# Merged operands ahead of the norm's casts, and a last down step with all operands kept, its products by halves of the positions

## The chip, the core and the metric

The kernel runs on one core of one Trainium2 chip. The core has a matrix engine (TensorE, PE in the profile; its weight loads are listed apart as PEld), a vector engine (VectorE, DVE), a scalar engine (ScalarE, ACT), a general engine (GpSimd, POOL) and a queue engine that issues the DMA transfers here (SyncE, SP). Each engine works through its own instructions in the order of the program and waits on semaphores for the others. Two on-chip memories matter: SBUF for operands and PSUM, in banks, for the sums of the matmuls.

The metric is the device time of one execution in microseconds (us), lower being better. All times of one profile count from the start of its span, the time from the first to the last instruction.

## The reference

One layer of an encoder block on 1040 positions (16 meta tokens and 1024 of the input) of 1024 channels, in float32. Two token mixers are merged by gates, the result is projected, normed and added to the residual; then comes a gated feed-forward part with a depthwise convolution of three taps, normed and added too.

```python
gates = jax.nn.sigmoid((gate_logits + b_gates[l]).reshape(bn, L, N_BRANCHES, D_MODEL))
merged = gates[:, :, 0] * y_a + gates[:, :, 1] * y_b
mix_out = merged @ w_out[l]
h_res = h_res + rmsnorm(mix_out, g_mix_post[l])

h2 = rmsnorm(h_res, g_ffn_pre[l])
up = centred_dwconv(h2 @ w_up[l], conv_w_ffn[l], conv_b_ffn[l])
a, v = jnp.split(up, 2, axis=-1)
ffn_out = (jax.nn.gelu(a) * v) @ w_down[l]
h_res = h_res + rmsnorm(ffn_out, g_ffn_post[l])
```

The output is `h_res` without the 16 meta tokens.

## The kernel before

Channels lie on the 128 partitions, positions on the free axis. A float32 operand of a matmul is split into a high half, a cast to `float32r` on ACT (L132), and a low half, the operand minus its high half, on DVE (L133). `mm3` (L160 to L168) then makes three matmuls of a product: high weights by high operand (L164), high by low (L166), low by high (L168). One level of a Strassen-Winograd scheme makes the large products out of seven half-sized ones (steps 0 to 6).

Two places of the program are touched.

**The out projection** (`project`, L958 ff.) computes `merged @ w_out` in four chunks of 258, 258, 258 and 256 positions (`CHM`). A chunk has eight tiles of 128 output channels (`mo`), each a sum over eight input tiles `kt`, that is 24 matmuls. After each tile ACT squares it (`sq_m`, L929) and scales it out of PSUM into `hA` or `hB` (L983, the eviction); DVE adds the squares. Hooks after a tile issue other work. With chunk `c` these are:

- after tile 0 the loads of the merged values of chunk `c + 1` into the three raw buffers (`mr`, `load_merged`);
- after tile 1 `norm_a(c - 1)`: the root of the mean, the scaling, the residual and the squares of the next norm;
- after tile 5 the splits of the first three (`MORE`) of the next chunk's eight merged operands (`mh` and `ml`, `split_merged`);
- after tile 6 the mean of the second norm (`mean_b`, one pair of matmuls into `ms_h`) and `norm_b(c - 1)`: three steps on DVE for the inverse root, eight scalings (L1028) and four casts with subtractions into `b11` and `b21`, operands of the feed-forward part;
- after tile 7 the splits of the other five merged operands, ordered by `issue_after` behind the last cast of `b11` (`cast`, `last_parts`).

Chunk `c + 1` can begin with the first three operands and needs the fourth after nine matmuls.

**The down projection** runs its steps in the order 0, 2, 4, 1, 3, 5, 6. Every step is a sum over eleven `k` (`NK`) with four output tiles each: 44 products of three matmuls over 512 positions, with the sums of steps 4, 3 and 6 in the PSUM banks `dna`, of step 5 in `dnb`. `operands` loads the gated values of two `k` into a raw buffer (`g`, three buffers of 512 KB), and splits weights (`wd`) and values (`gd`) into a ring of seven slots, so splits run some three `k` ahead of PE. Weights lie in rooms, large tiles named by `places`, two per room.

Step 6 is the last. Its first seven `k` run over all 512 positions. The last four (`LATE`) are split into rooms of their own (`late`) and multiplied by halves of 256 positions (`CUT`), so that the first half is complete before the second. Positions are output in two halves of 512: `finish(1, ...)` scales the second half of the positions (`z12`, `z22`), adds the residual (`hr`) and stores, after the mean that PE makes behind `k = 1`; `finish(0, ...)` does so for the first half of the positions (`z11`, `dn_u`), in two parts of 256.

```python
    load_residual(1, NK + 1)
    down(6, A, range(2))
    end = finish(1, mean(1), [(V, f, 1) for f in range(KT)])
    down(6, A, range(2, NK - LATE))
```

A recording layer with its own scheduler sets the final order on each engine; `behind` (`issue_after`) puts a group of instructions behind a named one.

Of the kernel before, what the change touches and what calls it, by code (L numbers as in the profile page):

```python
# [91 lines left out]
def block_kernel(ctx, tc, xT, x_res, w_u, w_in, w_fa, w_fa2, w_fb, w_fb2, w_co, w_out, w_up, w_dn,  # L92
# [861 lines left out]
    def split_merged(c, ks):  # L954
        for kt in ks:
            merged[c].append(merged_parts(c, kt, merged_r[c, kt // 3 * 3][:, kt % 3])[0])

    def project(c, hooks, order=range(KT)):  # L958
        n = CHM[c][1]
        sq = squares(f"m{c}", n)  # L960
        next(sq)
        outs = {}

        ahead = 5 if c == 0 else 0

        def mm(f, kt):
            if f not in outs:
                outs[f] = bank(f"mo{c}_{f}")[:, :n]
            mh, ml = merged[c][kt]
            with behind(*newest):  # L970
                mm3([outs[f]], tuple(t[:, kt * P : (kt + 1) * P] for t in wres[f]), ([mh], [ml]), kt == 0, kt == KT - 1)

        with behind(*done):
            while len(wres) < KT:
                out_weights(len(wres))
        for f in range(ahead):
            for kt in range(KT - 1):
                mm(f, kt)
        for n_, f in enumerate(order):
            for kt in range(KT - 1 if f < ahead else 0, KT):  # L980
                mm(f, kt)
            sq.send(outs[f])
            S.mul(h_at(c, f), outs[f], col("g_post", f))  # L983
            if n_ in hooks:
                with behind(*newest):
                    hooks[n_]()
        z[c] = sq
# [32 lines left out]
    def norm_b(c):  # L1020
# [5 lines left out]
        for f in range(KT):  # L1026
            h = h_at(c, f)
            V.scalar_tensor_tensor(out=h, in0=h, scalar=col("g_fpre", f), in1=rr, op0=ALU.mult, op1=ALU.mult)  # L1028
            if f % 2 == 0:
                continue  # L1030
            f -= 1
            if c < 2:
                a, e = max(c0, 1), min(c0 + n, NH + 1)
                got = put2(
                    hx["b11" if f < 4 else "b21"], f % 4, hA[f // 4][:, f % 4 : f % 4 + 2, a:e], a - 1, e - a
                )
                cast[:] = got[:1] if f < 4 else cast
            elif f < 4:
                sub(A(f), h_two(c, f), A(f))
                put2(hx["t1"], f, A(f), c0 - 513, n)  # L1040
            else:
                put2(hx["b22"], f - 4, B(f), c0 - 513, n)


    cast = []

    def second(c):
        j, n = CHM[c][0] - 513, CHM[c][1]
# [165 lines left out]
        psum_s.close()  # L1214
        psum_s, psum = scope("psum3", 6, space=PSUM)

    def last_parts(c):

        with behind(*cast):
            split_merged(c, range(MORE, KT))  # L1220

    project(0, {
        3: lambda: load_merged(1), 4: new_banks, 5: lambda: split_merged(1, range(MORE)),
        7: lambda: last_parts(1),
    })
    for c in range(1, 4):
        hooks = {
            0: lambda: load_merged(c + 1), 1: lambda: norm_a(c - 1), 5: lambda: split_merged(c + 1, range(MORE)),
            6: lambda: (mean_b(c - 1), norm_b(c - 1)), 7: lambda: last_parts(c + 1),
        }  # L1230
        order = range(KT)
        if c == 3:
# [99 lines left out]
    ssum = [fn.tile([P, HALF], F32, name=f"ss{i}") for i in range(2)]  # L1332
    A = [bank(f"dna{f}", firsts_) for f in range(4)]
    B = [bank(f"dnb{f}", None if f < 2 else seconds) for f in range(4)]
    LATE = 4
    AHEAD = 3
    CUT = 256
    PART0 = [(V, f, 1) for f in range(KT)]
    PART1 = [(V, 6, 1), (V, 0, 1), (V, 1, 1), (V, 2, 2), (V, 7, 1), (V, 4, 2)]
    gs = {}  # L1340
    hr = []

    def scr(name):
        return fn.tile([P, HALF], F32, tag="rs", name=name, bufs=3)
# [62 lines left out]
        rsqrt_of(f"r4_{half}_{o}", scr, ms, n, rr)  # L1407
        return rr

    def load_residual(half, at):  # L1410
        hr[:] = [tiles_in(at + i, f"hr{half}{i}") for i in range(2)]
        h0 = NM - TM + half * HALF
        for i in range(2):
            at = 0
            for c in (2 * half, 2 * half + 1):
                a = h0 + at - CHM[c][0]
                n = min(CHM[c][1] - a, HALF - at)
                SP.dma_start(hr[i][:, :, at : at + n], hres_d[c, :, 4 * i : 4 * i + 4, a : a + n])
                at += n
            assert at == HALF  # L1420

    def finish(half, rr, work, o=0, n=HALF):

        at = slice(o, o + n)
        for e, f, m in work:
# [21 lines left out]
    for f in range(4):  # L1447
        add(z22[:, f], A[f], z22[:, f])
        square(1, f + 4, z22[:, f])
    down(5, B)  # L1450
    for f in range(4):
        add(z12[:, f], B[f], u[:, f])
        square(1, f, z12[:, f])
    load_residual(1, NK + 1)
    down(6, A, range(2))
    end = finish(1, mean(1), [(V, f, 1) for f in range(KT)])
    down(6, A, range(2, NK - LATE))
    late = []
    for k in range(NK - LATE, NK):
        r = room(places[k - NK + LATE], F32R, f"late{k}")  # L1460
        into = [(r[:, i : i + 512], r[:, i + 512 : i + 1024]) for i in (0, 1024)]
        late.append((k, *operands(6, k, into)))
    list(end)
    load_residual(0, LATE)
    end = iter(())
    for o, n in ((0, CUT), (CUT, HALF - CUT)):
        at = slice(o, o + n)
        for f in range(4):
            next(end, None)
            for k, w, g in late:  # L1470
                mm(6, A, f, k, w, g, at)
            summed = add(u[:, f, at], A[f][:, at], u[:, f, at])
            rest = square(0, f + 4, u[:, f, at], o, n, last=f == 3)
            if f == 3:
                rr = mean(0, o, n, [rest])
                S.mul(u[:, f, at], u[:, f, at], col("g_fpost", f + 4))
        with behind(summed):
            list(end)
        end = finish(0, rr, PART0 if o == 0 else PART1, o, n)
    list(end)  # L1480
    dn_s.close()
    hx_s.close()
# [105 lines left out]
```

## Time and profile before

| | |
|---|---|
| time, median of 3 runs | 1212.87 us (1210.99 to 1213.8) |
| profiled execution, its own time | 1209.85 us |
| its span, first to last instruction | 1207.9 us |
| mean granted TensorE clock | 0.988 |
| out projection (PE works on `mo`) | 422.6 to about 531 us |
| down projection, step 6 on PE | 1159.98 to 1192.65 us |

The profile is of one execution. A row of a timeline gives the start, the duration, the engine, the line of the kernel, the operation, the tile written and the tiles read (buffer numbers left out), the shape, and in brackets the idle time of that engine just before, with what ended it. Rows of several equal instructions in a row are joined, with their count. A window's row gives the busy time of each engine in it. Matmuls are pipelined: the distance between two starts is what one costs, and it is shorter than the duration of one.

### The profile page before, as it was taken

The page shows a single profiled execution, that of the slowest core. Times are in us where ns is not written, and L with a number is a line of the kernel's source. Part 1 is how long each engine was busy: PE and PEld are TensorE (multiplying, and loading weights), DVE is VectorE, ACT ScalarE, POOL GpSimd, SP SyncE. Part 2 cuts the span into 40 slices and gives each one's busy share as a digit, 9 for nine tenths or more (in the row PEclk, how much of TensorE's full clock was granted, in tenths as well). Part 3 has the DMA queues.
Part 4 walks back from the last instruction along what each step waited for, and adds up shares of the span by engine and source line. Part 5 has one row for each costly group of instructions (what it writes and reads, how often), then busy time and mean ns, then how long its engine had stood idle before and what let it go on. Part 6 is the DMA issues. An engine that isn't in the chain of part 4 may idle for free.

```text
span 1207.9 us, 22189 instructions
## 1 busy us (share of the span) xinstructions
PE 1176.8 (97%) x8790; PEld 1134.4 (94%) x8790; DVE 997.4 (83%) x1685; ACT 549.1 (45%) x988; POOL 8.7 (1%) x41
## 2 busy tenths in 40 slices
PE   8999999999999998899999999999999999999995
PEld 7999999999999998899999999999999998888884
DVE  8999876756588857799799999989988989856678
ACT  6743343223443254456544544444344444455562
POOL 0000000000020000000000000000000000000000
PEclk9999999999999998899999999999999999999998
DMA  6336655132967853334243334323212499354433
GB/s 250 123 119 216 194 172 172 57 128 91 293 214 235 273 152 110 108 107 163 97 138 108 117 129 149 123 97 132 97 71 96 137 330 317 101 167 125 136 119 140
DMA packets 79215, 184.26 MB, mean 153 GB/s; under 512 B 7954, under 2 KB 25586, under 8 KB 79112
## 3 DMA queue, kind: packets, MB, share of 16 engines
q1 hardware_dynamic: 78968, 182.73, 46.2%
q8 instruction: 69, 1.13, 0.4%
q14 instruction: 34, 0.28, 0.1%
q10 hardware_dynamic: 144, 0.12, 0.0%
HBM read 131.55 MB, written 51.27 MB: 151 GB/s over the span
## 4 chain that ended last, share of the span: by engine, by line
PE 52%; DVE 4%; ACT 1%; DMA 1%; issue 0%; DVEq 0%; SPq 0%; ACTq 0%
PE up_d L168 3%; PE up_c L166 3%; PE up_c L164 3%; PE up_d L164 3%; PE up_d L166 3%; PE up_c L168 3%; PE up_a L164 3%; PE up_a L168 3%; PE up_a L166 3%; PE dna L166 3%; PE dna L164 3%; PE dna L168 3%; PE dnb L166 2%; PE dnb L164 2%; PE dnb L168 2%; PE up_b L168 2%
## 5 line engine op out<-in xcount | busy, mean ns | idle before, releaser
L166 PE MATMUL mo<-ml,wo 128*128 128x258 f32 (+1 forms) x256 | 74.5, 291 | 6.0 <-DVE ml L133 6.0
L164 PE MATMUL mo<-mh,wo 128*128 128x258 f32 (+1 forms) x256 | 75.5, 295 | 2.5 <-ACT mh L132 2.5
L168 PE MATMUL mo<-mh,wo 128*128 128x258 f32 (+1 forms) x256 | 74.1, 289 | 0.0
L166 PEld LDWEIGHTS mo<-ml,wo 128*128 128x128 f32 x256 | 50.7, 198 | 6.5 <-DVE ml L133 6.3
L164 PEld LDWEIGHTS mo<-mh,wo 128*128 128x128 f32 x256 | 50.5, 197 | 3.1 <-ACT mh L132 2.9
L168 PEld LDWEIGHTS mo<-mh,wo 128*128 128x128 f32 x256 | 50.5, 197 | 0.0
L132 ACT CAST up_1h<-up_1t 128x512 fp32r<-128x512 f32 x11 | 6.8, 622 | 74.9 <-DVE up_1t L149 44.6
L1160 ACT ACTIVATE up_0o<-up_0o 128x512 f32<-128x512 f32 x44 | 27.8, 631 | 23.7 <-DVE up_0o L1158 23.4
L1156 ACT ACTIVATE up_1o<-up_1x,pr 128x512 f32<-128x512 f32 x33 | 26.9, 816 | 23.0 <-DVE up_1x L149 22.5
L168 PE MATMUL up_d<-b22h,up_5l 128*128 128x258 f32 (+1 forms) x168 | 34.2, 284 | 0.0
L166 PE MATMUL up_c<-t3l,up_3h 128*128 128x258 f32 (+1 forms) x168 | 34.1, 285 | 0.0
L168 PE MATMUL up_b<-t2h,up_2l 128*128 128x258 f32 (+1 forms) x168 | 34.0, 283 | 0.0
L164 PE MATMUL up_d<-b22h,up_5h 128*128 128x258 f32 (+1 forms) x168 | 33.9, 283 | 0.0
L166 PE MATMUL up_d<-b22l,up_5h 128*128 128x258 f32 (+1 forms) x168 | 33.9, 283 | 0.0
L166 PE MATMUL up_b<-t2l,up_2h 128*128 128x258 f32 (+1 forms) x168 | 33.9, 283 | 0.0
L164 PE MATMUL up_c<-t3h,up_3h 128*128 128x258 f32 (+1 forms) x168 | 33.8, 282 | 0.0
L164 PE MATMUL up_b<-t2h,up_2h 128*128 128x258 f32 (+1 forms) x168 | 33.8, 282 | 0.0
L164 PE MATMUL up_c<-t4h,up_6h 128*128 128x258 f32 (+1 forms) x168 | 33.8, 282 | 0.0
L164 PE MATMUL up_d<-t1h,up_1h 128*128 128x258 f32 (+1 forms) x168 | 33.7, 282 | 0.0
L168 PE MATMUL up_d<-t1h,up_1l 128*128 128x258 f32 (+1 forms) x168 | 33.7, 282 | 0.0
L168 PE MATMUL up_c<-t3h,up_3l 128*128 128x258 f32 (+1 forms) x168 | 33.6, 281 | 0.0
L166 PE MATMUL up_d<-t1l,up_1h 128*128 128x258 f32 (+1 forms) x168 | 33.6, 281 | 0.0
(1337 smaller groups left out, 4295.8 us busy)
## 6 DMA issues: line engine op xcount, KB each, us to landing
g<-gp_d SPq DMA_DIRECT2D x35, 512.0 KB, 3.6
up_1r<-in_w_up_dram SPq DMA_DIRECT2D x22, 512.0 KB, 3.6
gp_d<-up_0o SPq DMA_DIRECT2D x44, 256.0 KB, 2.0
up_0r<-in_w_up_dram SPq DMA_DIRECT2D x20, 512.0 KB, 3.9
s<-sig_d SPq DMA_DIRECT2D x16, 514.0 KB, 6.2
sig_d<-g_s SPq DMA_DIRECT2D x30, 257.0 KB, 3.4
u<-fold_d SPq DMA_DIRECT2D x8, 777.0 KB, 4.2
fold_d<-fold SPq DMA_DIRECT2D x8, 521.0 KB, 3.3
```

Source lines behind the costliest of these rows:

```text
L132: a = copy(hi, src)
L164: nc.tensor.matmul(o, wh, h, start=first, stop=False, **kw)
L166: nc.tensor.matmul(o, wh, l, start=False, stop=False, **kw)
L168: newest[:] = [nc.tensor.matmul(o, wl, h, start=False, stop=last, **kw).ins]
L1156: S.activation(t, ap[:, 1 : 1 + HALF], AF.Identity, bias=col("cb_ffn", b), scale=w(1))
L1160: S.activation(t, t, AF.Gelu_apprx_tanh)
```

## The change

Nothing of what is computed changes. In the out projection all eight splits of the next chunk's merged operands are issued before `norm_b`, the first three behind the eviction of tile 5 (hook 5), the other five behind the eviction of tile 6 (hook 6, between `mean_b` and `norm_b`). `last_parts` and `cast` go.

In the down projection all eleven pairs of step 6's operands are kept, ten in rooms and the last in the ring. Five are prepared among the `k` of step 5, as their rooms come free, two after it and the rest within step 6. Step 6 runs all its `k` over the first 256 positions for the four tiles together, then over the second 256 positions tile by tile, each tile with all eleven `k`. The `finish` of the second half of the positions is issued with one tile per `k`, and the first half's residual is loaded into a tile of its own (`hr00`) and one room. `finish(0, ...)` works on two tiles at a time for all tiles.

```diff
@@ project
-            S.mul(h_at(c, f), outs[f], col("g_post", f))
+            evicted[:] = [S.mul(h_at(c, f), outs[f], col("g_post", f)).ins]
...
-    def last_parts(c):
-
-        with behind(*cast):
-            split_merged(c, range(MORE, KT))
+    def parts(c, ks):
+
+        with behind(*evicted):
+            split_merged(c, ks)
...
-            0: lambda: load_merged(c + 1), 1: lambda: norm_a(c - 1), 5: lambda: split_merged(c + 1, range(MORE)),
-            6: lambda: (mean_b(c - 1), norm_b(c - 1)), 7: lambda: last_parts(c + 1),
+            0: lambda: load_merged(c + 1), 1: lambda: norm_a(c - 1), 5: lambda: parts(c + 1, range(MORE)),
+            6: lambda: (mean_b(c - 1), parts(c + 1, range(MORE, KT)), norm_b(c - 1)),
@@ down projection
-    LATE = 4
     AHEAD = 3
     CUT = 256
-    PART0 = [(V, f, 1) for f in range(KT)]
-    PART1 = [(V, 6, 1), (V, 0, 1), (V, 1, 1), (V, 2, 2), (V, 7, 1), (V, 4, 2)]
+
+    EASY = 5
+    TWOS = [(V, f, 2) for f in range(0, KT, 2)]
...
-    down(5, B)
+
+
+    late = []
+
+    def last_operands(k):
+        into = (None, None)
+        if k < NK - 1:
+            r = room(places[k], F32R, f"late{k}")
+            into = [(r[:, i : i + 512], r[:, i + 512 : i + 1024]) for i in (0, 1024)]
+        late.append(operands(6, k, into))
+
+    for k in range(NK):
+        down(5, B, [k])
+        if k % 2 and k // 2 < EASY:
+            last_operands(k // 2)
     for f in range(4):
         add(z12[:, f], B[f], u[:, f])
         square(1, f, z12[:, f])
-    load_residual(1, NK + 1)
-    down(6, A, range(2))
-    end = finish(1, mean(1), [(V, f, 1) for f in range(KT)])
-    down(6, A, range(2, NK - LATE))
-    late = []
-    for k in range(NK - LATE, NK):
-        r = room(places[k - NK + LATE], F32R, f"late{k}")
-        into = [(r[:, i : i + 512], r[:, i + 512 : i + 1024]) for i in (0, 1024)]
-        late.append((k, *operands(6, k, into)))
+    res = load_residual(1, [tiles_in(NK + 1 + i, f"hr1{i}") for i in range(2)])
+    last_operands(EASY)
+    last_operands(EASY + 1)
+    for k in range(NK):
+        if EASY + 1 < k + 2 < NK and k + 2 >= len(late):
+            last_operands(k + 2)
+        for f in range(4):
+            mm(6, A, f, k, *late[k], slice(0, CUT))
+        if k == 0:
+            end = finish(1, mean(1), [(V, f, 1) for f in range(KT)], res)
+        else:
+            next(end, None)
+        if k == 4:
+            res0 = load_residual(0, [fn.tile([P, 4, HALF], F32, name="hr00"), tiles_in(NK + 1, "hr01")])
     list(end)
-    load_residual(0, LATE)
     end = iter(())
     for o, n in ((0, CUT), (CUT, HALF - CUT)):
         at = slice(o, o + n)
         for f in range(4):
-            next(end, None)
-            for k, w, g in late:
-                mm(6, A, f, k, w, g, at)
-            summed = add(u[:, f, at], A[f][:, at], u[:, f, at])
+            if o:
+                for k in range(NK):
+                    mm(6, A, f, k, *late[k], at)
+            add(u[:, f, at], A[f][:, at], u[:, f, at])
             rest = square(0, f + 4, u[:, f, at], o, n, last=f == 3)
             if f == 3:
                 rr = mean(0, o, n, [rest])
                 S.mul(u[:, f, at], u[:, f, at], col("g_fpost", f + 4))
-        with behind(summed):
-            list(end)
-        end = finish(0, rr, PART0 if o == 0 else PART1, o, n)
+            else:
+                next(end, None)
+                next(end, None)
+        end = finish(0, rr, TWOS, res0, o, n)
     list(end)
```

What stands where on DVE at the end of chunk 1 of the out projection, before the change (`r3_0` and `rrb0` are the second norm of chunk 0, `sq_m1_7` the square of chunk 1's tile 7, `ml2_3` and on the low halves of chunk 2's operands):

```order
L174 SCALAR_TENSOR_TENSOR r3_0_t_5746<-r3_0_y_5745 128x258
L175 SCALAR_TENSOR_TENSOR r3_0_t_5746<-ms_h0_5742,r3_0_t_5746 128x258
L176 SCALAR_TENSOR_TENSOR rrb0_5744<-r3_0_t_5746,r3_0_y_5745 128x258
L1028 SCALAR_TENSOR_TENSOR hA0_5160<-hA0_5160,pr_67,rrb0_5744 128x258 x4
L133 TENSOR_TENSOR b11l_5167<-hA0_5160,b11h_5166 128x2x257
L1028 SCALAR_TENSOR_TENSOR hA1_5161<-hA1_5161,pr_67,rrb0_5744 128x258
L133 TENSOR_TENSOR b11l_5167<-hA0_5160,b11h_5166 128x2x257
L1028 SCALAR_TENSOR_TENSOR hA1_5161<-hA1_5161,pr_67,rrb0_5744 128x258 x3
L149 TENSOR_TENSOR sq_m1_0_5495<-sq_m1_0_5495,sq_m1_7_5792 128x258
L133 TENSOR_TENSOR b21l_5169<-hA1_5161,b21h_5168 128x2x257 x2
L133 TENSOR_TENSOR ml2_3_5797<-mr2_3_5500,mh2_3_5796 128x258
L133 TENSOR_TENSOR ml2_4_5801<-mr2_3_5500,mh2_4_5800 128x258
```

The same place of the changed program:

```order
L174 SCALAR_TENSOR_TENSOR r3_0_t_5766<-r3_0_y_5765 128x258
L133 TENSOR_TENSOR ml2_3_5745<-mr2_3_5500,mh2_3_5744 128x258
L133 TENSOR_TENSOR ml2_4_5749<-mr2_3_5500,mh2_4_5748 128x258
L133 TENSOR_TENSOR ml2_5_5753<-mr2_3_5500,mh2_5_5752 128x258
L133 TENSOR_TENSOR ml2_6_5757<-mr2_6_5502,mh2_6_5756 128x258
L133 TENSOR_TENSOR ml2_7_5761<-mr2_6_5502,mh2_7_5760 128x258
L175 SCALAR_TENSOR_TENSOR r3_0_t_5766<-ms_h0_5742,r3_0_t_5766 128x258
L176 SCALAR_TENSOR_TENSOR rrb0_5764<-r3_0_t_5766,r3_0_y_5765 128x258
L149 TENSOR_TENSOR sq_m1_0_5495<-sq_m1_0_5495,sq_m1_7_5812 128x258
L1031 SCALAR_TENSOR_TENSOR hA0_5160<-hA0_5160,pr_67,rrb0_5764 128x258 x4
L133 TENSOR_TENSOR b11l_5167<-hA0_5160,b11h_5166 128x2x257
```

The five subtractions have moved from behind the eight scalings and four subtractions of the norm to right behind its first step. At the start of chunk 3 it reads alike.

On PE, the mean of the second half of the positions (`ms4_1_0`) in step 6, before the change and, in the second fence, after it (`late2` holds the operands of `k = 2`):

```order
L164 MATMUL dna3_12106<-gd6_1h_13667,wd6_1h_13663 128x512
L166 MATMUL dna3_12106<-gd6_1l_13668,wd6_1h_13663 128x512
L168 MATMUL dna3_12106<-gd6_1h_13667,wd6_1l_13664 128x512
L1405 MATMUL ms4_1_0_13683<-ss1_12102,ones_69 128x512
L164 MATMUL dna0_12103<-gd6_2h_13699,wd6_2h_13695 128x512
```

```order
L168 MATMUL dna1_12104<-late2_13516 128x256
L164 MATMUL dna2_12105<-late2_13516 128x256
L1401 MATMUL ms4_1_0_13701<-ss1_12102,ones_69 128x512
L166 MATMUL dna2_12105<-late2_13516 128x256
L168 MATMUL dna2_12105<-late2_13516 128x256
```

The mean stood behind 24 matmuls of 512 positions and now stands behind 31 of 256.

On DVE, the end of step 5's splits before the change (`wd6_0` and on are the weights of step 6, `z12` the sum that closes step 5):

```order
L133 TENSOR_TENSOR wd5_10l_13594<-wd_b22h_12096,wd5_10h_13593 128x512
L133 TENSOR_TENSOR gd5_10l_13598<-g5_10_13590,gd5_10h_13597 128x512
L133 TENSOR_TENSOR wd6_0l_13643<-wd_t2l_12091,wd6_0h_13642 128x512
L133 TENSOR_TENSOR gd6_0l_13647<-g6_0_13639,gd6_0h_13646 128x512
L133 TENSOR_TENSOR wd6_1l_13664<-wd_t3h_12092,wd6_1h_13663 128x512
L133 TENSOR_TENSOR gd6_1l_13668<-g6_0_13639,gd6_1h_13667 128x512
L149 TENSOR_TENSOR z12_12097<-dnb0_12107,dn_u_12099 128x512
```

And after it:

```order
L133 TENSOR_TENSOR wd5_10l_13630<-wd_b22h_12096,wd5_10h_13629 128x512
L133 TENSOR_TENSOR late6_13681<-g6_6_13682,late6_13681 128x512
L133 TENSOR_TENSOR late7_13776<-g6_6_13682,late7_13776 128x512
L133 TENSOR_TENSOR gd5_10l_13634<-g5_10_13626,gd5_10h_13633 128x512
L133 TENSOR_TENSOR wd6_10l_13845<-wd_b22h_12096,wd6_10h_13844 128x512
L133 TENSOR_TENSOR late8_13797<-g6_8_13798,late8_13797 128x512
L133 TENSOR_TENSOR late9_13820<-g6_8_13798,late9_13820 128x512
L133 TENSOR_TENSOR gd6_10l_13849<-g6_10_13841,gd6_10h_13848 128x512
L149 TENSOR_TENSOR z12_12097<-dnb0_12107,dn_u_12099 128x512
```

Every operand of step 6 is now split before `z12`; no split is left between `z12` and the last store.

More of the change, by code (lines that the diff above doesn't have):

```diff
@@ L956, in split_merged @@
             merged[c].append(merged_parts(c, kt, merged_r[c, kt // 3 * 3][:, kt % 3])[0])
+    evicted = []
     def project(c, hooks, order=range(KT)):
@@ L1033, in norm_b @@
                 a, e = max(c0, 1), min(c0 + n, NH + 1)
[L1034 to L1037, printed above, removed]
+                put2(hx["b11" if f < 4 else "b21"], f % 4, hA[f // 4][:, f % 4 : f % 4 + 2, a:e], a - 1, e - a)
             elif f < 4:
@@ L1042, in norm_b @@
                 put2(hx["b22"], f - 4, B(f), c0 - 513, n)
-    cast = []
     def second(c):
@@ L1215, in new_banks @@
         psum_s, psum = scope("psum3", 6, space=PSUM)
-    def last_parts(c):
-        with behind(*cast):
-            split_merged(c, range(MORE, KT))
+    def parts(c, ks):
+        with behind(*evicted):
+            split_merged(c, ks)
     project(0, {
-        3: lambda: load_merged(1), 4: new_banks, 5: lambda: split_merged(1, range(MORE)),
-        7: lambda: last_parts(1),
+        3: lambda: load_merged(1), 4: new_banks, 5: lambda: parts(1, range(MORE)),
+        6: lambda: parts(1, range(MORE, KT)),
     })
@@ L1334, in block_kernel @@
     B = [bank(f"dnb{f}", None if f < 2 else seconds) for f in range(4)]
-    LATE = 4
     AHEAD = 3
     CUT = 256
-    PART0 = [(V, f, 1) for f in range(KT)]
-    PART1 = [(V, 6, 1), (V, 0, 1), (V, 1, 1), (V, 2, 2), (V, 7, 1), (V, 4, 2)]
+    EASY = 5
+    TWOS = [(V, f, 2) for f in range(0, KT, 2)]
     gs = {}
-    hr = []
     def scr(name):
@@ L1408, in mean, with load_residual @@
         return rr
-    def load_residual(half, at):
-        hr[:] = [tiles_in(at + i, f"hr{half}{i}") for i in range(2)]
+    def load_residual(half, tiles):
         h0 = NM - TM + half * HALF
-        for i in range(2):
+        for i, t in enumerate(tiles):
             at = 0
@@ L1417, in load_residual, with finish @@
                 n = min(CHM[c][1] - a, HALF - at)
-                SP.dma_start(hr[i][:, :, at : at + n], hres_d[c, :, 4 * i : 4 * i + 4, a : a + n])
+                SP.dma_start(t[:, :, at : at + n], hres_d[c, :, 4 * i : 4 * i + 4, a : a + n])
                 at += n
             assert at == HALF
-    def finish(half, rr, work, o=0, n=HALF):
+        return tiles
+    def finish(half, rr, work, hr, o=0, n=HALF):
         at = slice(o, o + n)
```

## The prediction

> **What bounds the kernel now.** I read the page first, then the table by windows for the two places that the change touches, then the timelines of each engine there. The page gives the span and the shares of the busiest engines.
>
> ```profile
> span 1207.9 us, 22189 instructions
> PE 1176.8 (97%) x8790; PEld 1134.4 (94%) x8790; DVE 997.4 (83%) x1685; ACT 549.1 (45%) x988; POOL 8.7 (1%) x41
> ```
>
> PE is idle for 31.1 us only (1207.9 - 1176.8), so the change can win where PE waits or after PE's last work. The windows of 10 us (columns: window, length, then busy time of PE, PEld, DVE, ACT, POOL, granted clock, DMA share, GB/s) show two holes in the out projection:
>
> ```profile
> 470.00:480.00 10.00, 5.76 (x29) 5.36 (x29) 7.73 (x19) 5.96 (x16) 0.21 (x2) 0.66 0.29 81
> ...
> 500.00:510.00 10.00, 5.80 (x32) 5.39 (x31) 7.39 (x18) 4.86 (x13) 0.00 (x0) 0.70 0.22 67
> ```
>
> PE's timeline (start, duration, line, tile, idle time before and its releaser) at the start of chunks 2 and 3:
>
> ```profile
> 467.79 0.28 PE L164 MATMUL mo<-mh,wo 128*128 128x258 f32 x1
> 470.53 0.28 PE L168 MATMUL mo<-mh,wo 128*128 128x258 f32 x1
> 472.07 0.38 PE L164 MATMUL mo<-mh,wo 128*128 128x258 f32 x1 [1.26 <-ACT mh L132]
> 475.43 0.58 PE L166 MATMUL mo<-ml,wo 128*128 128x258 f32 x1 [2.98 <-DVE ml L133]
> 480.07 0.28 PE L166 MATMUL mo<-ml,wo 128*128 128x258 f32 x1
> ...
> 501.24 0.28 PE L168 MATMUL mo<-mh,wo 128*128 128x256 f32 x1
> 510.75 0.28 PE L166 MATMUL mo<-ml,wo 128*128 128x256 f32 x1
> ```
>
> From 467.79 to 470.53 lie 23 matmul steps in 2.74 us. The next 23 steps, 470.53 to 480.07, take 9.54: the two waits, then 21 matmuls at about 0.213 us instead of 0.119 while the window shows clock 0.66. **Each hole costs 9.54 - 2.74 = 6.80 us**; the second, 501.24 to 510.75, 9.51 - 2.74 = 6.77. Together 13.57.
>
> What ends the wait is DVE's subtraction for the low half of the merged operands:
>
> ```profile
> 467.62 0.43 DVE L174 SCALAR_TENSOR_TENSOR r_t<-r_y 128x258 f32<-128x258 f32 x1 [0.30 <-ACT r_y L173]
> ...
> 474.95 2.78 DVE L133 TENSOR_TENSOR ml<-mr,mh 128x258 fp32r<-128x258 f32 x8
> ```
>
> DVE runs the second norm of the chunk before (from 467.62) ahead of them.
>
> The other place is the end:
>
> ```profile
> 1157.27 0.39 PE L164 MATMUL dnb<-gd_10h,wd_10h 128*128 128x512 f32 x1
> ...
> 1159.98 0.39 PE L164 MATMUL dna<-gd_0h,wd_0h 128*128 128x512 f32 x1
> 1165.20 0.40 PE L168 MATMUL dna<-gd_1h,wd_1l 128*128 128x512 f32 x1
> 1165.43 1.02 PE L1405 MATMUL ms<-ss,ones 128*128 128x512 f32 x2
> 1179.92 0.28 PE L164 MATMUL dna<-late 128*128 128x256 f32 x1
> 1187.34 0.28 PE L164 MATMUL dna<-late 128*128 128x256 f32 x1
> 1187.76 0.70 PE L1405 MATMUL ms<-ss,ones 128*128 128x256 f32 x2
> 1194.84 0.70 PE L1405 MATMUL ms<-ss,ones 128*128 128x256 f32 x2 [2.19 <-DVE ss L149]
> ```
>
> The last product ends 2.19 ahead of the last row, at 1192.65, and the span at 1207.9, so 15.25 us of tail follow, in which DVE still has both halves to finish:
>
> ```profile
> 1152.45 0.69 DVE L133 TENSOR_TENSOR gd_10l<-g,gd_10h 128x512 fp32r<-128x512 f32 x1 [1.43 <-ACT gd_10h L132]
> 1158.50 1.88 DVE L149 TENSOR_TENSOR z<-dnb,dn_u 128x512 f32<-128x512 f32 x3
> 1162.70 1.48 DVE L149 TENSOR_TENSOR ss<-ss,dsq 128x512 f32<-128x512 f32 x2
> 1175.27 1.28 DVE L155 TENSOR_TENSOR z<-z,rr 128x512 f32<-128x512 f32 x2
> 1184.90 1.08 DVE L149 TENSOR_TENSOR dn_u<-dna,dn_u 128x256 f32<-128x256 f32 x3
> 1195.04 0.42 DVE L149 TENSOR_TENSOR dn_u<-dna,dn_u 128x256 f32<-128x256 f32 x1
> 1197.20 0.43 DVE L174 SCALAR_TENSOR_TENSOR r_t<-r_y 128x256 f32<-128x256 f32 x1
> 1203.50 1.02 DVE L149 TENSOR_TENSOR dn_u<-dn_u,hr 128x256 f32<-128x256 f32 x2
> ```
>
> **Part one, the operands ahead of the norm's casts.**
>
> ```profile
> 471.62 1.32 ACT L132 CAST mh<-mr 128x258 fp32r<-128x258 f32 x4
> ```
>
> Nothing is added or removed; the eight splits of a chunk move. The first three now follow the eviction of tile 5, the other five follow the mean's matmul and the norm's first step. On ACT the three casts put 3 x 0.33 = 1.0 us (1.32 / 4 each) ahead of the eviction of tile 6, the other five follow it. DVE then does the five subtractions right behind the row at 467.62: at 2.78 / 8 = 0.35 us each, plus about 0.3 that the earlier three push them, the first is ready near 468.7 and the fifth near 470.1. PE wants the first at 470.65, one step after 470.53, so some 1.9 us of cover hide them; were it gone, each microsecond late would cost one. Both waits go, and with them the slow clock: **-13.57**. Their loads are no obstacle: three of these subtractions stand far earlier in the program already.
>
> [...]
>
> What is late next: the norm, by the 1.7 us of the five, and DVE behind it.
>
> ```profile
> 498.30 0.43 DVE L174 SCALAR_TENSOR_TENSOR r_t<-r_y 128x258 f32<-128x258 f32 x1 [0.31 <-ACT r_y L173]
> 505.63 1.76 DVE L133 TENSOR_TENSOR ml<-mr,mh 128x256 fp32r<-128x256 f32 x5
> 510.79 1.29 DVE L133 TENSOR_TENSOR pw<-up_0p0er,pw 128x512 fp32r<-128x512 f32 x2 [3.40 <-ACT pw L132]
> 513.44 0.43 DVE L149 TENSOR_TENSOR sq_m<-sq_m,sq_m 128x256 f32<-128x256 f32 x1 [1.36 <-ACT sq_m L929]
> 524.79 0.42 DVE L149 TENSOR_TENSOR sq_h<-sq_h,sq_h 128x258 f32<-128x258 f32 x1
> 527.39 0.60 PE L937 MATMUL ms_h<-sq_h,ones 128*128 128x258 f32 x2
> ```
>
> DVE's idle of 3.40 and 1.36 us is the second hole's mirror image; without it DVE's work must fit beside PE's. From 498.30, which comes 6.7 earlier (491.6), DVE has 7.33 us of norm, 1.76 of operands and 0.6 of pw until the square of 513.44: 501.3, 12.1 earlier, and a second pw behind it leaves 11.5. PE comes 13.57 earlier, so DVE lags by about 2.1 us. The mean at 527.39 needs the sum of 524.79 (ready 525.21): slack 2.18. So the lag is just hidden; I charge 0.3, near the hidden end since lag and slack meet (the ends are 0 and 2.1). Part one: **-13.3**.
>
> **Part two, the last down step.** PE's pace: 5.22 us for 23 steps from 1159.98, 0.227 each with 512 positions; 7.42 us for 63 steps from 1179.92, 0.1178 with 256. Before, 84 x 0.227 + 96 x 0.1178 = 30.4 us; now 264 x 0.1178 = 31.1: +0.7.
>
> Step 5 now carries 17 of step 6's 22 splits among its own (the other five stand in step 3, where four stood). DVE has 46 instructions of 0.602 us there, 27.7 us, against 11 x 2.72 = 29.9 us of PE. The loads behind them (3.6 us to land, row below) go out as raw buffers come free; by that order the last two reach their casts near 1154 and 1155 and the last split ends near 1156.7, ahead of the z adds at 1158.50, which wait for PE. I cost it at nothing; if that cover of 1.8 us went, the z adds would move, and the end one for one.
>
> ```profile
> g<-gp_d SPq DMA_DIRECT2D x35, 512.0 KB, 3.6
> 1162.79 0.61 ACT L1395 ACTIVATE dsq<-z 128x512 f32<-128x512 f32 x1
> 1166.62 1.28 ACT L173 ACT_TABLE_LOAD   x1
> 1167.92 0.69 ACT L173 ACTIVATE r_y<-ms,eps_t 128x512 f32<-128x512 f32 x1
> ```
>
> Two waits are new. (1) The mean of the second half stands behind 31 half-size matmuls instead of 24 full ones: PE reaches it at 1159.98 + 31 x 0.1178 = 1163.63, the sum is ready at 1164.18: 0.55 us, then 0.87 for the mean itself; the first half of the products ends at 1176.95. (2) DVE's chain: mean done 1165.2, table load beside it, 0.69 for the root, three steps of 0.70, and 16 finishing instructions of 0.602 (1175.27 to 1184.90 before) end at 1177.8. No casts lie between them any more; that is 7.1 us earlier than 1184.90. The next mean follows 2.86 us behind (1187.76 - 1184.90), at 1180.65. PE, 20 matmuls into its second half, is there at 1179.3 and waits 1.35. Queued behind it are 112 matmuls: 0.97 for the mean, 13.2, last end **1195.0 instead of 1192.65**.
>
> The tail gets shorter: the first half is finished under those 13 us. Behind the last product stand the add, square, mean and root (2.2 us from add to first step, as now), three steps of 0.43, then eight instructions of 0.60 (the form of 1175.27): 1195.05 + 3.5 + 4.9 = 1203.45, where the same point was 1204.52. The 3.38 us of last transfer remain. Part two: **-1.05**. With both waits hidden it would be -3; with the z adds 2 us late, +1.
>
> **Sum.** -13.3 - 1.05 = -14.35: a span of 1193.55. The profiled execution took 1209.85, which gives 1195.5; the median of the runs shown is 1212.87, 3.0 above it, so I take **1198.5**.
>
> **Rivals.**
> - *DVE becomes the bound behind chunk 3* (20%). For it: the lag of 2.1 us meets a slack of 2.18, and DVE is dense from 514 on. Against it: small idle times later absorb it. All of the lag is paid: 1200.4.
> - *The new waits of step 6 drop the clock* (10%). One slow phase costs 21 x 0.095 = 2.0: 1200.5. Against it: 2.19 us of idle at 1194.84 left the mean at 0.70, as at 1187.76. [...]
> - *The waits of step 6 are hidden* (8%), if the sums come sooner: 1196.5.
> - *The holes stay* (4%): the five splits still land behind the norm's casts, only part two is won, 1211.8. The order of the built program speaks against it.
> - *Slower* (3%): step 5 starves. ACT takes its queue in order, and twelve loads now share three raw buffers, six of them for step 6. If one of those stands unlanded at the head, step 5's casts wait behind it. A step's last low half is ready at 1153.14 (1152.45 + 0.69) and used at 1157.27, so 4.1 us are covered, about one landing of 3.6; from two landings in a row PE pays. If five of the six did that, 5 x 3.6 = 18 us go, more than is won: 1216. No wait of PE in step 5 of the trace points to it.
>
> **How the numbers follow.** The forecast has 55%. The range takes in the lag (+1.9), a slow phase (+2.0), hidden waits (-2) and the 3 us between the profiled run and the median: 1193.5 to 1204.5. A difference under 0.2% (2.4 us) is no difference for this kernel. Faster 0.93, same 0.04, slower 0.03.
>
> **What would show it.** No idle time in front of mo at chunks 2 and 3 and clock 1.00 in those windows; ms_h of chunk 2 within 0.5 us of its neighbours; a wait of about 0.5 us before the first ms of step 6 and 1.4 before the second; last product some 2.3 us later relative to step 6's start, the tail behind it near 11.8 us instead of 15.25. I am wrong if mo waits for ml again, or if step 5 shows waits for gd or late.

## The result, and the profile after

The changed kernel took **1196.20 us** (median of 4 executions, 1194.83 to 1198.36), the kernel before 1211.93 (median of 4, 1209.70 to 1213.80): a ratio of **0.9873**, 95% interval 0.9848 to 0.9897. The profiled execution took 1195.46 us, 14.39 less than the 1209.85 of before; its span is 14.6 shorter. The page of the changed kernel gives the span and PE's busy time:

```profile
span 1193.3 us, 22307 instructions
PE 1172.6 (98%) x8874; PEld 1134.3 (95%) x8874; DVE 996.9 (84%) x1673; ACT 549.5 (46%) x988; POOL 8.7 (1%) x41
```

PE is idle for 20.7 us (1193.3 - 1172.6) where it was 31.1. The windows of 10 us that held the two holes (window, length, busy time of PE, PEld, DVE, ACT, POOL, granted clock, DMA share, GB/s) are full now:

```profile
470.00:480.00 10.00, 10.00 (x84) 9.95 (x83) 9.78 (x22) 4.87 (x11) 0.08 (x1) 1.00 0.25 69
500.00:510.00 10.00, 10.00 (x87) 10.00 (x86) 10.00 (x20) 4.91 (x13) 0.00 (x0) 1.00 0.50 127
```

DVE's timeline of the changed kernel at the start of chunk 2 (start, duration, line, tile, idle time before it and its releaser):

```profile
467.80 0.43 DVE L174 SCALAR_TENSOR_TENSOR r_t<-r_y 128x258 f32<-128x258 f32 x1 [0.19 <-ACT r_y L173]
468.15 1.77 DVE L133 TENSOR_TENSOR ml<-mr,mh 128x258 fp32r<-128x258 f32 x5
469.84 0.42 DVE L175 SCALAR_TENSOR_TENSOR r_t<-ms_h,r_t 128x258 f32<-128x258 f32 x1
...
501.06 0.42 DVE L149 TENSOR_TENSOR sq_m<-sq_m,sq_m 128x256 f32<-128x256 f32 x1
...
511.95 0.95 DVE L149 TENSOR_TENSOR sq_h<-sq_h,sq_h 128x258 f32<-128x258 f32 x2
```

The five subtractions stand right behind the first step of the root and end at 469.92; PE wants the first at 470.94 (next fence). The row at 501.06 is the first square added in chunk 3; the last row is the sum for the second norm's mean of chunk 2, ready at 512.90.

PE's timeline there, and from the start of step 6 to its last product:

```profile
470.94 0.29 PE L166 MATMUL mo<-ml,wo 128*128 128x258 f32 x1
...
513.98 0.60 PE L937 MATMUL ms_h<-sq_h,ones 128*128 128x258 f32 x2
...
1146.55 0.28 PE L164 MATMUL dna<-late 128*128 128x256 f32 x1
...
1150.12 0.28 PE L164 MATMUL dna<-late 128*128 128x256 f32 x1
1150.39 1.12 PE L1401 MATMUL ms<-ss,ones 128*128 128x512 f32 x2
...
1151.59 0.28 PE L164 MATMUL dna<-late 128*128 128x256 f32 x1
...
1163.24 0.28 PE L168 MATMUL dna<-gd_10h,wd_10l 128*128 128x256 f32 x1
1164.69 0.38 PE L164 MATMUL dna<-late 128*128 128x256 f32 x1 [1.17 <-DVE dn_u L149]
...
1167.16 0.62 PE L1401 MATMUL ms<-ss,ones 128*128 128x256 f32 x2
...
1181.15 0.28 PE L168 MATMUL dna<-gd_10h,wd_10l 128*128 128x256 f32 x1
```

The mean of chunk 2 has no idle time in front of it: PE comes 1.08 us after the sum (513.98 - 512.90). Step 6 starts 13.43 us earlier than before (1159.98 - 1146.55), so about that is what part one gave. From there to the end are 46.75 us (1193.3 - 1146.55), where 47.92 were (1207.9 - 1159.98): part two gave 1.17. In step 6 PE waits once, 1.17 us in front of the first product of the second half. DVE's timeline of the same stretch says why:

```profile
1142.81 0.69 DVE L133 TENSOR_TENSOR gd_10l<-g,gd_10h 128x512 fp32r<-128x512 f32 x1 [0.22 <-ACT gd_10h L132]
1144.70 2.05 DVE L149 TENSOR_TENSOR z<-dnb,dn_u 128x512 f32<-128x512 f32 x3 [1.20 <-PE dnb L168]
...
1163.01 1.29 DVE L149 TENSOR_TENSOR z<-z,hr 128x512 f32<-128x512 f32 x2
1164.22 1.08 DVE L149 TENSOR_TENSOR dn_u<-dna,dn_u 128x256 f32<-128x256 f32 x3
```

The adds that empty the banks of step 6 (`dn_u<-dna`) stand on DVE behind the 16 finishing instructions; the first of them starts at 1164.22 and releases PE. Both halves of a tile lie in one bank of 512 positions, and PE's first product of the second half waits 1.17 us for the add that reads the first (`<-DVE dn_u L149`). The first two rows show that the splits of step 6 cost nothing in step 5: the last is done at 1143.50, and DVE then waits 1.20 us for PE before the z adds.

### The profile page after: what moved, and what is told of

Its sections match the earlier page's. It is cut to its first block, busy times and chain, and to the rows that moved or that the text cites. A ratio compares the mean times of both kernels' runs of the same rounds, so it can differ in the third digit from the quotient of the medians.

```text
span 1193.3 us, 22307 instructions
## 1 busy us (share of the span) xinstructions
PE 1172.6 (98%) x8874; PEld 1134.3 (95%) x8874; DVE 996.9 (84%) x1673; ACT 549.5 (46%) x988; POOL 8.7 (1%) x41
## 3 DMA queue, kind: packets, MB, share of 16 engines
q8 instruction: 70, 1.15, 0.4%
## 4 chain that ended last, share of the span: by engine, by line
PE 81%; DVE 10%; DMA 3%; ACT 3%; issue 1%; SPq 0%; DVEq 0%; ACTq 0%
PE up_d L168 3%; PE up_c L166 3%; PE up_c L164 3%; PE up_d L164 3%; PE up_d L166 3%; PE up_c L168 3%; PE dna L164 3%; PE dna L168 3%; PE dna L166 3%; PE up_a L164 3%; PE up_a L168 3%; PE up_a L166 3%; PE dnb L168 2%; PE dnb L166 2%; PE dnb L164 2%; PE mo L164 2%
## 5 line engine op out<-in xcount | busy, mean ns | idle before, releaser
L164 PE MATMUL mo<-mh,wo 128*128 128x258 f32 (+1 forms) x256 | 73.5, 287 | 0.0
L168 PE MATMUL mo<-mh,wo 128*128 128x258 f32 (+1 forms) x256 | 72.2, 282 | 0.0
L164 PEld LDWEIGHTS mo<-mh,wo 128*128 128x128 f32 x256 | 48.5, 189 | 0.2
L168 PEld LDWEIGHTS mo<-mh,wo 128*128 128x128 f32 x256 | 48.6, 190 | 0.0
```

The source lines that it names most:

```text
L164: nc.tensor.matmul(o, wh, h, start=first, stop=False, **kw)
L168: newest[:] = [nc.tensor.matmul(o, wl, h, start=False, stop=last, **kw).ins]
```

## The experiments

The part of the program before the out projection is the same in all kernels, yet its length varied by 3.3 us between the traces. So the parts are measured from marks of their own. All numbers (us) are starts in the traces, from PE's rows of mo and dna; the last column is the span less the start of step 6.

| kernel | first mo | last mo | out projection | start of step 6 | step 6 to the end |
|---|---|---|---|---|---|
| before | 422.6 | 530.3 | 107.7 | 1159.98 | 47.92 |
| the change | 422.8 | 516.9 | 94.1 | 1146.55 | 46.75 |
| out projection alone | 423.2 | 517.4 | 94.2 | 1146.56 | 47.84 |
| down step alone | 422.9 | 531.0 | 108.1 | 1160.54 | 46.76 |
| the five alone | 424.8 | 519.0 | 94.2 | 1149.27 | 46.73 |
| the three alone | 424.6 | 532.0 | 107.4 | 1161.71 | 47.79 |
| holes filled | 423.4 | 527.1 | 103.7 | 1156.17 | 48.43 |
| holes filled in part | 425.1 | 530.2 | 105.1 | 1160.69 | 48.41 |
| more work on DVE | 425.9 | 521.4 | 95.5 | 1151.62 | 46.78 |
| two tiles held back | 425.6 | 519.7 | 94.1 | 1149.47 | 45.33 |
| cut at 384 | 424.5 | 518.7 | 94.2 | 1148.31 | 50.09 |
| two finishes on POOL | 423.0 | 517.1 | 94.1 | 1147.32 | 46.48 |

In both kernels with filled holes step 6 to the end is 0.5 us longer than before; no run was made to find out why.

**The out projection alone.** The kernel before with the new order of the splits and the old last down step:

```
...
-            0: lambda: load_merged(c + 1), 1: lambda: norm_a(c - 1), 5: lambda: split_merged(c + 1, range(MORE)),
-            6: lambda: (mean_b(c - 1), norm_b(c - 1)), 7: lambda: last_parts(c + 1),
+            0: lambda: load_merged(c + 1), 1: lambda: norm_a(c - 1), 5: lambda: parts(c + 1, range(MORE)),
+            6: lambda: (mean_b(c - 1), parts(c + 1, range(MORE, KT)), norm_b(c - 1)),
...
```

> The kernel before with the moved splits of the out projection alone; the end is as before. Theory (both holes are the wait for the five subtractions plus the slow clock behind it, 13.5 us in all, and nothing behind them is bound by DVE): span 1207.9 - 13.5 = 1194.4, no idle time of PE before mo, and behind the last product a tail of 15.2 us as before. Rival (the gain needs the new end too, or DVE becomes the bound once the holes are gone): span 1196.5 or more, with PE idle before ms_h or up_a.

Span 1194.4, ratio 0.9877 (0.9854 to 0.9899). Step 6 starts at 1146.56, as in the change, and takes 47.84, as before. The moved splits gain 13.4 us by themselves.

**The down step alone.** The kernel before with the new last step, its out projection untouched.

> The kernel before with the new last down step alone; the out projection is as before. Theory: both holes stay (13.5 us), the end wins what it won in the change, about 1.1 us: span 1206.8, with 1.2 us of idle before the first product of the second half and a tail of about 12.0 us. Rival (the end is worth more or less when the holes stand, because loads and buffers come at other times): a span outside 1206.3 to 1207.4.

Span 1207.3, ratio 0.9986 (0.9975 to 0.9997). Step 6 begins 0.56 later than before (the start 0.3, the out projection 0.4, the rest -0.1). From there to the end are 46.76 us, within 0.01 of the change. So the parts add up: 13.4 and 1.2, and the end does not depend on the holes.

**The five alone.** The changed kernel, the first three splits of a chunk where they stood:

```
...
-            0: lambda: load_merged(c + 1), 1: lambda: norm_a(c - 1), 5: lambda: parts(c + 1, range(MORE)),
+            0: lambda: load_merged(c + 1), 1: lambda: norm_a(c - 1), 5: lambda: split_merged(c + 1, range(MORE)),
...
```

> The changed kernel, with the first three splits of each chunk where they stood before (no longer tied to the eviction of tile 5); only the last five stay ahead of the norm. Theory (PE waited for the fourth operand of a chunk, and only the order of the five on DVE decides): both holes stay away, span 1193.3 within 0.5. Rival (the three casts of the early splits hold up ACT's evictions, and their place is part of the gain): a wait of PE for an eviction or for mh comes back, 1 us or more per chunk, span 1195 or more.

The span is 1196.0, outside what the theory gave; the ratio is 0.9894 (0.987 to 0.9918). But the difference does not lie in the out projection, which takes 94.2 us and shows no idle time of PE: 2.0 of the 2.7 come before the first mo and 0.6 behind the last. To close the holes, the five are enough. That the whole kernel is as fast as the change is not shown: its median is 1199.01, 2.8 us above, with four executions of each.

**The three alone.** The kernel before, the first three splits behind the eviction of tile 5, the last five behind the norm's casts as before:

```
...
-            0: lambda: load_merged(c + 1), 1: lambda: norm_a(c - 1), 5: lambda: split_merged(c + 1, range(MORE)),
+            0: lambda: load_merged(c + 1), 1: lambda: norm_a(c - 1), 5: lambda: parts(c + 1, range(MORE)),
...
```

> The kernel before with only the first three splits of each chunk moved behind the eviction of tile 5; the last five stay behind the norm's casts, and the end is as before. Theory: nothing is won, both holes of 6.8 us stay, since PE waits for the first of the five: span 1207.9 within 0.5. Rival (the three early splits delay the norm's first step, so moving them shortens or lengthens the holes by their 1.1 us each): 1205.7 or 1210.1.

Span 1209.5, ratio 0.9991 (0.9978 to 1.0005). The out projection takes 107.4 us: both holes are there. The 1.6 us more of span are the start again (424.6 against 422.6). PE's timeline in the hole of chunk 2:

```profile
474.15 0.38 PE L164 MATMUL mo<-mh,wo 128*128 128x258 f32 x1 [1.29 <-ACT mh L132]
477.51 0.39 PE L166 MATMUL mo<-ml,wo 128*128 128x258 f32 x1 [2.97 <-DVE ml L133]
...
478.21 0.40 PE L164 MATMUL mo<-mh,wo 128*128 128x258 f32 x1
...
481.64 0.29 PE L166 MATMUL mo<-ml,wo 128*128 128x258 f32 x1
```

The waits are those of before (1.26 and 2.98), but the slow clock begins 0.7 us after the second and lasts 3.4 us: 16 steps at 0.21 (478.21 to 481.64), where the prediction counted 21 in the trace of before. So a hole's slow phase differs between executions with the same waits; here it costs 1.5 us (16 x 0.095) and not 2.0.

**Holes filled.** Is the slow clock behind a hole brought by the idle time? The kernel before with work for PE in it:

```
             for kt in range(KT - 1 if f < ahead else 0, KT):
                 mm(f, kt)
+                if c >= 2 and n_ == 0 and kt == MORE - 1:
+                    g = order[1]
+                    outs[g] = bank(f"mo{c}_{g}")[:, :n]
+                    for _ in range(36):
+                        with behind(*newest):
+                            newest[:] = [
+                                nc.tensor.matmul(
+                                    outs[g], wres[f][0][:, :P], merged[c][0][0], start=True, stop=True
+                                ).ins
+                            ]
```

> The kernel before, with 36 matmuls whose result is overwritten put into each of the two holes, between the third and the fourth operand of chunks 2 and 3; no split is moved. At 0.119 us they take 4.3 us, about as long as the two waits of a hole (1.26 + 2.98). Theory (a hole is 4.7 us of waiting, set by DVE, and 2.0 us of slow clock that comes from the idle time): the fourth operand comes when it came, and the 21 matmuls behind it run at 0.119 us instead of 0.213; each hole costs 4.7 instead of 6.8, and from the first to the last product of the out projection there are 103.7 us instead of 107.7. Rival (the slow pace has another cause than the idle time): no change, 107.7, or more by what the added matmuls delay.

PE's timeline in the hole of chunk 2:

```profile
471.49 4.48 PE L988 MATMUL mo<-mh,wo 128*128 128x258 f32 x36
...
476.27 0.39 PE L166 MATMUL mo<-ml,wo 128*128 128x258 f32 x1 [0.19 <-DVE ml L133]
476.50 0.29 PE L168 MATMUL mo<-mh,wo 128*128 128x258 f32 x1
476.62 0.29 PE L164 MATMUL mo<-mh,wo 128*128 128x258 f32 x1
```

The low half still comes when DVE gets to it, but the matmuls behind it follow at 0.12 us, with clock 1.00 in the window from 470 to 480 us. The out projection takes 103.7 us, to the tenth what was expected; ratio 0.9961 (0.9945 to 0.9976). **Adding 72 useless matmuls made the out projection 4 us shorter, and the kernel faster.** A hole of before was 2.0 us of slow clock (4.0 for two) and 4.8 of waiting, for ACT's cast and then for DVE's subtraction (9.6 for two, which the change takes off as well: 103.7 to 94.1).

**Holes filled in part.** The same with 12 matmuls in chunk 2 and 22 in chunk 3:

```
-                    for _ in range(36):
+                    for _ in range(12 if c == 2 else 22):
```

> The kernel before with the overwritten matmuls again, but 12 of them in the hole of chunk 2 (1.4 us) and 22 in that of chunk 3 (2.6 us), so that idle stretches of about 2.9 and 1.7 us are left in one piece. The question is how much idle time brings the slow clock. Theory A (one idle stretch of about 3 us or more does it): chunk 2 shows 21 matmuls or so at 0.213 us, chunk 3 none; from the first to the last product of the out projection 105.7 us. Theory B (it takes the 4.2 us of the whole hole): neither is slow, 103.7 us. Theory C (what counts is how much of a longer window PE is idle, and where the window's edge falls): slow phases shorter or later than those of the kernel before, or in one chunk only and not the same in each execution.

PE's timeline behind each of the two waits, and the windows over the first:

```profile
477.89 0.39 PE L166 MATMUL mo<-ml,wo 128*128 128x258 f32 x1 [2.97 <-DVE ml L133]
478.11 0.28 PE L168 MATMUL mo<-mh,wo 128*128 128x258 f32 x1
...
478.95 0.41 PE L164 MATMUL mo<-mh,wo 128*128 128x258 f32 x1
479.16 0.42 PE L166 MATMUL mo<-ml,wo 128*128 128x258 f32 x1
...
482.38 0.29 PE L166 MATMUL mo<-ml,wo 128*128 128x258 f32 x1
...
508.08 0.39 PE L166 MATMUL mo<-ml,wo 128*128 128x256 f32 x1 [1.88 <-DVE ml L133]
508.30 0.28 PE L168 MATMUL mo<-mh,wo 128*128 128x256 f32 x1
```

```profile
470.00:480.00 10.00, 7.03 (x54) 6.80 (x53) 9.82 (x24) 5.33 (x15) 0.20 (x2) 0.95 0.05 3
480.00:490.00 10.00, 10.00 (x75) 9.95 (x74) 5.02 (x11) 2.95 (x8) 0.00 (x0) 0.88 0.38 127
```

Behind an idle stretch of 2.97 us came the slow clock, behind one of 1.88 it did not, each seen once. But the slow clock came a microsecond after the work had begun again and lasted 3.4 us (16 steps, 478.95 to 482.38). In that time 1.7 us of clock are missing (0.05 and 0.12 of 10 us), so it is half speed; in the hole of chunk 2 before, the windows from 474 to 479 us show clock 0.50. By the same measure that hole had 6.8 us of it (0.34 of 10 us, times two), some 2.2 of them while PE still waited, since its rows are slow from 475.43 to 480.07 only; the window from 473 to 474 us, in which PE does nothing, shows 0.59 already. So theory A fits which hole was slow, and C that the phase came later and was shorter, as the hole of "the three alone" also shows; that a longer window decides it, as C has it, is not shown. The timed ratio is 1.000 (0.9984 to 1.0016): the 2.6 us that this trace gains in the out projection are not seen over the 8 executions. How often a hole brings no, one or two such phases is open.

**More work on DVE.** The changed kernel, nine instructions more in chunk 2:

```
         rr = rs[c]
+        if c == 1:
+            for i in range(9):
+                add(scratch(f"junk{i}")[:, :n], rr, rr)
```

> The changed kernel with nine more instructions of 0.34 us on DVE (3.1 us, results unused) between the norm's root and its scaling in chunk 2. In the changed kernel the sum for the mean of chunk 2's second norm is ready 1.1 us ahead of PE. Theory (this is the whole slack; DVE has no idle time between): PE waits 2.0 us at that mean, and the end of the out projection comes 2.0 us later. Rival 1 (DVE was the bound already): 3.1 us later. Rival 2 (the order of DVE's work absorbs it): no change.

PE's timeline at the mean, and where the added delay shows again 45 us later, with the row of the changed kernel that answers to the second behind it:

```profile
518.37 0.70 PE L937 MATMUL ms_h<-sq_h,ones 128*128 128x258 f32 x2 [1.09 <-DVE sq_h L149]
...
563.51 0.51 PE L164 MATMUL up_a<-b21h,ep 128*128 128x258 f32 x2 [1.14 <-ACT up_u L295]
```

```profile
558.46 0.51 PE L164 MATMUL up_a<-b21h,ep 128*128 128x258 f32 x2 [0.58 <-ACT up_u L295]
```

The out projection is 1.4 us longer (95.5), and the second wait, 0.58 in the changed kernel, is 1.14: together 2.0. From the first mo to the start of step 6 are 725.7 us against 723.75, again 2.0; ratio 0.9901 (0.9878 to 0.9924). So 1.1 of the 3.1 us were slack. The theory's sum is right, its place only for two thirds of it.

**Two tiles held back.** The changed kernel, part of the finishing work put behind the adds:

```
-        else:
+        elif k < 6:
             next(end, None)
...
-    list(end)
+    held = end
...
                 rr = mean(0, o, n, [rest])
                 S.mul(u[:, f, at], u[:, f, at], col("g_fpost", f + 4))
+                list(held)
```

> The changed kernel; DVE finishes the second half of the positions in another order: two of the eight tiles are held back behind the adds and the sum of the new step's first half. In the changed kernel PE waits 1.2 us (1.33 with the gap in the pace) before the first product of the second half, for the add that empties its bank; that add is queued on DVE behind all 16 finishing instructions. Theory: this queue is the whole wait; with four of the instructions behind it the wait is 0 and the last product and the end come 1.3 us earlier: from the start of step 6 to the end of the span 45.4 us instead of 46.75. Rival (what is held back comes due later, in the tail, since DVE must still do it before the last finish): the wait goes and the tail of 12.0 us grows by as much, 46.7 us.

DVE's timeline where the adds stand now:

```profile
1163.52 1.29 DVE L149 TENSOR_TENSOR z<-z,hr 128x512 f32<-128x512 f32 x2
1165.41 1.14 DVE L149 TENSOR_TENSOR dn_u<-dna,dn_u 128x256 f32<-128x256 f32 x3 [0.60 <-PE dna L168]
```

Now DVE waits for PE. The wait of PE is gone, and step 6 to the end takes 45.33 us, 1.42 less than in the change. The tail did not grow: 12.2 us from the start of the last product (1182.60 to 1194.8), as in the change (1181.15 to 1193.3). The time, 1196.51 with a ratio of 0.9877 (0.9858 to 0.9896), cannot be told from that of the change, since this kernel's traced execution reached the out projection 2.8 us later. By the trace of the stretch this version is better; by the time it is not shown.

**Cut at 384.** The changed kernel with `CUT = 384` in place of 256.

> The changed kernel with the last step cut at 384 of 512 positions instead of 256. DVE's last chain shrinks: eight instructions of 0.60 us by about 0.25 each, and add, square, root and three steps by about 0.1 each: the tail of 12.0 us becomes about 9.5. Theory: PE's pace goes with the positions (0.227 us for 512, 0.118 for 256), so 132 matmuls of 384 take 132 x 0.172 = 22.7 us and 132 of 128 take 132 x 0.063 = 8.3 us, as much as before; from the start of step 6 to the end 44.5 us instead of 46.75. Rival (under 256 positions the pace stays at about 0.118 us a matmul, because the weights behind it load no faster): the second half takes 15.6 us, 7 us more, and the whole 51 us.

PE's rows near the end:

```profile
1180.90 0.28 PE L168 MATMUL dna<-late 128*128 128x128 f32 x1
...
1182.58 0.28 PE L168 MATMUL dna<-late 128*128 128x128 f32 x1
...
1189.61 0.28 PE L168 MATMUL dna<-gd_10h,wd_10l 128*128 128x128 f32 x1
```

Fifteen steps in 1.68 us: 0.112 each with 128 positions, hardly less than the 0.118 with 256. The tail is 8.8 us (1198.4 - 1189.61), 3.4 shorter than in the change, but the last product starts 6.7 later after the start of step 6 (41.30 for 34.60), and step 6 to the end takes 50.09; ratio 0.991 (0.989 to 0.993). The rival held, a little below its 51: a piece of 128 positions cost PE 0.112 us, nearly as much as one of 256. That the loading of the weights is the reason is not shown.

**Two finishes on POOL.** As "two tiles held back", and the first pair of tiles of the last finish on POOL:

```
-        end = finish(0, rr, TWOS, res0, o, n)
+        end = finish(0, rr, [*TWOS[1:], (nc.gpsimd, 0, 2)] if o else TWOS, res0, o, n)
```

> As e5_held, and of the last eight finishing instructions on DVE (0.60 us each) two, those of the first pair of tiles, go to POOL. Theory (DVE's finishing is the tail, and POOL works beside it): DVE has 1.2 us less to do; the tail of 12.2 us behind the last product becomes 11.0, if POOL's two instructions take no more than 3.6 us together, and from the start of step 6 to the end 44.1 us. Rival (POOL is slower than that, or slows DVE down beside it): POOL's transfer is the last one, and the tail is 12.2 us or longer.

DVE and POOL in the tail:

```profile
1184.39 0.69 DVE L155 TENSOR_TENSOR z<-z,rr 128x512 f32<-128x512 f32 x1
1185.00 1.75 DVE L155 TENSOR_TENSOR dn_u<-dn_u,rr 128x512 f32<-128x512 f32 x1
1186.67 1.74 DVE L149 TENSOR_TENSOR z<-z,hr 128x512 f32<-128x512 f32 x1
1188.34 0.68 DVE L149 TENSOR_TENSOR dn_u<-dn_u,hr 128x512 f32<-128x512 f32 x1
...
1184.49 1.71 POOL L155 TENSOR_TENSOR z<-z,rr 128x512 f32<-128x512 f32 x1 [714.19 <-DVE rr L176]
1186.28 1.59 POOL L149 TENSOR_TENSOR z<-z,hr 128x512 f32<-128x512 f32 x1
```

POOL takes 1.71 and 1.59 us, quick enough. DVE's row at 1184.39, which starts ahead of POOL's first, keeps its 0.69, but the two that start while POOL runs take 1.75 and 1.74. The tail is 13.35 us (1193.8 - 1180.45), 1.15 longer than with two tiles held back; the time (ratio 0.9874, 0.9848 to 0.99) does not resolve it. The rival held: beside POOL each of these two took DVE 1.67 us from start to start, where in "two tiles held back" it was 0.60.

## Why the prediction was right, by its steps

- **The holes, -13.57.** Right in size and cause. The out projection went from 107.7 to 94.1 us; the five alone do it, the three alone don't; a hole of before is 4.8 us of waiting and 2.0 of slow clock. That both holes had 2.0 belongs to that execution: in "the three alone" one had 1.5.
- **What is late next, +0.3.** The charge should have been nothing. The lag was worked out as 2.1 us against a slack of 2.18; the sum came 12.31 earlier (525.21 to 512.90) and PE 13.41 earlier (527.39 to 513.98), so the lag was 1.1 and a slack of 1.1 was left. The working had DVE 12.1 earlier at the first square of chunk 3 and, behind the second pw subtraction, 11.5; the square starts 12.38 earlier (513.44 to 501.06), and from there to the sum nothing more than 0.07 is lost (12.38 to 12.31): the second pw was taken up by DVE's small idle times and by the order of what follows. Nine more instructions showed the slack: 3.1 us of work cost 2.0. The rival that DVE becomes the bound was near, within 1.1 us of deciding.
- **Step 6, the first new wait.** The wait and the mean together were put at 0.55 + 0.87 = 1.42 in the first half and are 1.11: 1150.12 to 1151.59 is 1.47 for three steps, which take 0.36. The sum was ready 3.78 us after step 6 began (1149.64 + 0.69 - 1146.55), and not 4.20 as taken over from before (1164.18 - 1159.98), so of the 0.55 some 0.2 are left.
- **Step 6, the second new wait.** It has its size (1.35 predicted, 1.17 idle and 1.33 against the pace: 1164.69 - 1163.24 - 0.12) and its cause, DVE's 16 finishing instructions, but **not its place**. The prediction let PE run 20 matmuls into the second half and wait at the mean. PE stopped before the first of them: the product of tile 0 writes into the bank that the first add has yet to read. The prediction looked for whoever needs the sum and passed over who needs the bank. That the size came out the same is half luck. Both waits hang on the same queue on DVE, but the 20 matmuls from the one place to the other (2.4 us) also happen to take as long as DVE needs from the first add to the sum (1164.58 to 1167.02); the mean then started at 1167.16, without a wait. Holding back two tiles removed the wait.
- **The tail.** The last product starts 34.60 us after step 6 began (1181.15 - 1146.55), 32.40 before (1192.38 - 1159.98, the row below): +2.2, predicted +2.35. From its start to the end are 12.15 us instead of 15.52: -3.4, as predicted. Part two -1.17 for -1.05. No run takes the edits of part two apart (the order of the halves, the early splits, the finishing by pairs), so which of them shortens the tail is argued and not shown.

```profile
1192.38 0.28 PE L168 MATMUL dna<-late 128*128 128x256 f32 x1
```

- **Step 5 does not starve.** The last split was put 1.8 us ahead of the z adds and is 1.2 ahead (1143.50 and 1144.70). The prediction put 17 of step 6's 22 splits into step 5; between PE's start of it (1116.62) and the z adds DVE does 14, and eight earlier. That rival found no wait in the trace; where it would begin was not tried.
- **No slow clock in step 6.** Behind the wait of 1.17 us the next matmuls stand at 0.12, and the windows from 1165 to 1180 us show clock 1.00. No slow clock came behind the 1.88 us above either.
- **From the sum to the median.** The span was put at 1193.55 and is 1193.3, the execution's own time at 1195.5 and is 1195.46. The term of 3.0 us from there to the median is mis-sized: it was 0.74 (1196.20 - 1195.46), and the 2.3 us between 1198.5 and the result are this term alone. The 3.0 was one execution against the median of three. Before's profiled execution had the earliest start of the out projection of all twelve traces, and with the fourth execution the median of before is 2.1 above it (1211.93 - 1209.85). So the 3.0 depended on which few executions were at hand.

## What to carry to other kernels

A wait in the middle of dense matmuls can cost more than its length, as 4.8 us of waiting cost 6.8 here: find the order on the engine that ends it, count the slow matmuls behind it, and where the wait can't go, work that is thrown away can be cheaper than idle time, as the 72 matmuls were that took 4.0 us off the out projection. When a later stage writes into the same banks, ask of each new wait not only who needs the result, but who still reads the bank: in step 6 that was a wait of 1.17 us. Compare executions from a mark inside the program when the gain is smaller than the scatter of its start.

## What the runs showed of the hardware

**The slow clock came in pieces of 3.4 us.** The rows show one piece of 3.4 us in chunk 2 of the partly filled holes and one in chunk 2 of "the three alone"; the granted clock gives 6.8, two pieces, for the hole of chunk 2 before. The start of the program has such pieces too, where PE waits three times within 5 us (0.8 to 0.9, 1.5, and 0.3 to 0.8 us), and not in each execution. The windows from 20 to 30 us (length, PE's busy time, granted clock) of the kernel before, of the out projection alone, and of the kernel with more work on DVE:

```profile
20.00:30.00 10.00, 6.54 (x30) 0.83 0.23 81
```

```profile
20.00:30.00 10.00, 6.05 (x33) 1.00 0.23 82
```

```profile
20.00:30.00 10.00, 7.07 (x28) 0.72 0.27 93
```

That is one piece (0.17 of 10 us, times two), none, and two with what falls into the next window (0.28 and 0.07 of 10 us). With none or one the out projection began between 422.6 and 423.4 us, with two between 423.0 and 425.9: part of the scatter of the times, and not all of it. In the kernel before no single gap of PE from 20 to 30 us is longer than 1.53 us, and yet the slow clock came; in the out projection it came behind a gap of 2.97 and not behind one of 1.88. How much idle time brings it is not shown.

**POOL beside DVE.** Two DVE instructions of 128x512 took 1.75 us (`dn_u<-dn_u,rr`) and 1.74 (`z<-z,hr`) where they started while POOL ran one; the one that started ahead of POOL took 0.69, the first behind it 0.68. So POOL was no spare engine for this finish.

**Pace by positions.** In step 6 a matmul took PE 0.227 us with 512 positions (5.22 us for 23 steps), 0.118 with 256 (7.42 for 63) and 0.112 with 128 (1.68 for 15): from 256 to 128 only 0.006 us were gained.
